# First down group on the up-projection's banks, the sums' matmul six ticks further behind, and the mixers' decay tables behind further projection units

## The chip, the cores and the metric

One Trainium2 chip, one of its eight cores. The metric is the device time of one launch, in microseconds: the median of the runs of one kernel. One more execution was recorded by the profiler; all rows below come from it.

## The reference, cut to what matters

1024 frames of width 1024, with 16 meta tokens in front, go through two layers. The first layer's mixer is a gated DeltaNet ("GDN"), the second's an mLSTM; behind each mixer stands a feed-forward net ("FFN") with a causal convolution over three frames. Everything is float32.

```python
for i in range(DEPTH):                       # DEPTH = 2
    a_in = rms_norm(hs, norm_w[i, 0])
    mix = gated_deltanet(a_in, ...) if i % 2 == 0 else mlstm(a_in, ...)
    hs = hs + keep * rms_norm(mix, norm_w[i, 1])
    f = conv_ffn(rms_norm(hs, norm_w[i, 2]), ...)
    hs = hs + keep * rms_norm(f, norm_w[i, 3])

def gated_deltanet(h, ...):
    proj = h @ w_in                          # 1024 -> q, k, v, z and the gates
    g = -exp(a_log) * softplus(gates + dt_bias)
    G = cumsum(g)                            # the decay table, chunk by chunk
    decay = exp(G_i - G_j)                   # used by every chunk's products
    ...
    return (rms_norm(o, norm_w) * silu(z)) @ w_out

def mlstm(h, ...):
    proj = h @ w_in
    b = cumsum(log_sigmoid(gates))           # its decay table
    ...
    return (rms_norm(hh, norm_w) * o_gate) @ w_out

def conv_ffn(h, w_up, conv_w, conv_b, w_down):
    u = causal_depthwise_conv(h @ w_up, conv_w) + conv_b   # 1024 -> 2 x 2816, 3 taps
    gate, up = u[..., :2816], u[..., 2816:]
    return (silu(gate) * up) @ w_down                      # 2816 -> 1024
```

## The kernel before

**Tiles.** Features lie on the 128 partitions, frames along the free axis. Mixers work on 3 blocks of 348 columns. The out-projections and the FFN work on two halves t = 0 and 1 of 520 columns, each as two quarters n = 0 and 1 of 260. Every product is computed as three matmuls (lines 255 to 257: high part by high, low part by high, high part by low), and each weight tile is split first into its high part by ACT (L145) and its low part by POOL (L146).

**Layers and names.** Tiles of the GDN's out-projection have `go` in their names, those of the mLSTM's `mo`, those of the FFN's down-projection `f` (`dn_f`, `acc_f`, `so_f`), those of its up-projection `up` and `u`. The input of the mLSTM's projection is `xh_f`, `xl_f`, its projections are `pj_mi`, those of the GDN `pj_gi`.

**PSUM.** Eight banks under four tags, two each: `pj`, `pp`, `px`, `sp`. `next_bank` hands them out in turn: with `conv_banks` set it alternates between `pj` and `sp`, otherwise among `pj`, `pp` and `px`. While the up-projection runs, `conv_banks` is set, because the convolution accumulates its outputs `z` in `pp` and `px`: ACT writes the tap with the bias there (L1325), and VectorE adds the other two taps (L1327). An up-projection's bank is emptied into `u` by ACT (L1297) or, in the later columns j, where seven products are combined, by VectorE (L227).

**The FFN.** `ffn()` runs `up()` for 22 column tiles j; for j below 6 only the half t = 0 is computed at first (the plain form, four banks of 24 matmuls: `up_j_h_n`), later both halves together with seven products for eight. Then come the down groups (t, g): (0,0) contracts two tiles of the hidden features, the others four. A group has 16 outputs `dn_f_t_g_m_n`, each in a bank of its own, which VectorE copies (L484, g = 0) or adds (L486) to `acc_f`.

**Ticks and lags.** Work that follows an out- or down-projection is queued as jobs and emitted by `tick()`: a down bank of four tiles advances it by 2, one of the first group by 1, a plain up bank by 4, a bank of the seven-product form by 2, a unit of the mLSTM's projection by 5. At the end of a half's quarter the jobs are: the mean square of the mix (`fs_of`, `fs_ogo`, its rstd on ACT as Ln, L284, and Exp, L287); eight steps, two ticks apart, that add the residual (L378, L379) and accumulate the squares of the new stream in `ss` (L320 on ACT, L321 on VectorE); `LAG_PRE` ticks later the sums' matmul `fs_go`, `fs_mo` or `fs_f` (L328, two fp32 passes with a matrix of ones), and the factor `r` from it; and `LAG_OPS` = 2 ticks later the loads and splits of the next operands (`f_b` loaded in L1249, scaled in L1252, `b` and `t` cast by ACT in L1258 and completed by VectorE in L1259 and L1263). The up-projection reads `b` and `t`.

**Engines are in order.** What stands behind a waiting instruction on an engine waits too. A list scheduler places the emitted work on each engine; the rows under "The change" are its result.

**Decay tables.** In both mixers a generator `gates` computes the gates on VectorE step by step; its last step makes the running sum on TensorE (`cum_gdn`, `tot_gdn`, `cum_ml`, `tot_ml`, L584 and L588). The GDN takes that step before its first activation burst, the mLSTM before its units i = 2 and 3 of the projection.

Of the kernel before, what the change touches and what calls it, by code (L numbers as in the profile page):

```python
# [41 lines left out]

N_FIRST = 6

LAG_POST, LAG_N, LAG_PAGE, LAG_PRE, LAG_OPS = 6, 16, 2, 4, 2

LAST = ("f1", 1)

# [18 lines left out]
def weave(*parts):  # L67

    live = [[g, max(n, 1), 0] for g, n in parts]
    while live:  # L70
        p = min(live, key=lambda p: (p[2] + 0.5) / p[1])
        try:
            next(p[0])
            p[2] += 1
        except StopIteration:
            live.remove(p)


def run(g):
    for _ in g:  # L80
        pass
# [8 lines left out]
class Trunk:  # L90
# [560 lines left out]
    def gdn(self):  # L651
        a = self.a
        self.o_dram = [self.pd.tile([P, 2, TP], F32, tag=f"o_g_{h}", name=f"o_g_{h}", bufs=1) for h in range(NQK)]
        self.pages_of = {}
        self.blocks = {}
        n_all = NQK * NB
        tiles = lambda h: [h, NQK + h, 2 * NQK + 2 * h, 2 * NQK + 2 * h + 1, 32 + 2 * h, 32 + 2 * h + 1]

        def silu(h, tiles):
            self.burst([y for i in tiles for y in self.pages_of[h, i]], self.last, AF.Silu)  # L660

        def project(n):


            h, part = divmod(n, NB)
            i = (4, 0, 2)[part]
            g = h + (part > 0)
            yield from self.gdn_project(g, tiles(g)[i : i + 2], i)
            silu(g, (i, i + 1))

        def enter(b):
            hs = []
            for m in range(KD):
                h = self.page("C", f"hs_in_{b}_{m}", N_PAGES)
                sl = slice(b * BS, (b + 1) * BS)
                nc.sync.dma_start(h, self.hs[:, m, sl])
                self.put_input(h, m, sl)
                hs.append(h)
            return hs

        nc = self.nc
        t0 = tiles(0)
        weights = lambda t: self.split_weights(a["gdn_w_in"][t], f"gi{t}")
        self.new_input(0, "in")
        self.rt = self.new_factors("in")
        wg = self.split_weights(a["gdn_gate_w"], "gdn_gates", 32)
        hs = [enter(0)]
        ws = [weights(t0[0])]
        self.tables()
        hs.append(enter(1))  # L690
        ws.append(weights(t0[1]))
        hs.append(enter(2))
        rows = []
        for b in range(NB):
            acc = self.squares_now(hs[b], f"in{b}", None)
            self.now.append(lambda acc=acc, b=b: self.norm(acc, f"in{b}", self.r(b)))
            rows.append(self.gate_rows(wg, b, "gdn"))
            if b == NB - 1:
                gates = self.gdn_gates(rows)
                next(gates)  # L700
            for i in range(2):
                run(self.gdn_unit(0, i, t0[i], ws[i], b))
        lb, tb = next(gates)
        silu(0, (0, 1))
        order = t0[2:4] + [t for h in range(NQK) for t in tiles(h)[4:] + (tiles(h + 1)[:4] if h + 1 < NQK else [])]
        self.queue_weights([(a["gdn_w_in"][t], f"gi{t}") for t in order], 1)

        def first():
            yield from self.gdn_project(0, tiles(0)[2:4], 2)
            silu(0, (2, 3))  # L710

        weave((self.gdn_prepare(0, tb, lb), 13), (first(), 6))
        out = self.out_projection(a["gdn_w_out"], NQK, "go", GDN_CORE, GDN_LATE, 1, 2)
        for n in range(n_all):
            parts = [(self.gdn_recur(n, tb), 14)]
            if n + 1 < n_all:
                parts.insert(0, (self.gdn_prepare(n + 1, tb, lb), 27))
            if n:
                parts.append((self.gdn_finish(n - 1), 4))
            parts.append((project(n), 8) if n <= n_all - NB else (islice(out, 28), 28))  # L720
            weave(*parts)
        weave((self.gdn_finish(n_all - 1), 4), (out, 30))
# [341 lines left out]
    def mlstm(self):  # L1064
# [16 lines left out]
        for b in range(1, NB):  # L1081
            rows.append(self.gate_rows(wg, b, "ml"))
            if b == NB - 1:
                gates = self.ml_gates(rows)
                next(gates)
            for i in range(2):
                self.ml_unit(0, i, t0[i], ws[i], b)
                self.tick(5)
        li, tb = next(gates)
        self.queue_weights([(a["ml_w_in"][t], f"mi{t}") for t in t0[2:] + [t for h in range(1, ML_H) for t in tiles(h)]], 1)  # L1090
        for i in (2, 3):
            w = self.next_weights()
            for b in range(1, NB):
                self.ml_unit(0, i, t0[i], w, b)

        def first():
            for i in (4, 5):
                w = self.next_weights()
                for b in range(1, NB):
                    self.ml_unit(0, i, t0[i], w, b)  # L1100
                    yield
            self.burst([y for i in (4, 5) for y in self.pages_of[0, i]], self.last, AF.Sigmoid)
# [244 lines left out]
    def ffn(self, L, order, row, post, pre):  # L1347
        nc = self.nc
        name = f"f{L}"
        self.hidden = self.pd.tile([P, NF, NTOK], F32, tag=f"h_{L}", name=f"h_{L}", bufs=1)  # L1350

        src = lambda k, t: self.hidden[:, k, t * HB : (t + 1) * HB]
        place = lambda n: self.fp_page(n, F32R)
        seq = [(t, g) for t in range(2) for g in range(-(-NF // 4))]
        group, queue = self.second(name, NF, self.a["ffn_w_down"][L], src, place, seq, lambda t, n: self.end(t, n, post, pre, name, t == 1 and pre is not None))
        queue()
        while 0 not in self.xo:
            self.tick(1)
        self.hs, self.rt = self.new_hs, self.new_rt
        self.conv_banks, self.evicted = True, None  # L1360
        for j, halves in order:
            if 1 in halves and 1 not in self.xo:
                while 1 not in self.xo:
                    self.tick(1)
            self.up(L, j, halves)
        self.conv_banks = False
        for t, g in seq:
            run(group(t, g))
            if (t, g) == (1, 1) and pre is not None:
                self.new_input(pre, name)  # L1370
                for part in [z for p in self.xt for z in p]:
                    nc.gpsimd.memset(part[:, NTOK:].bitcast(F32), 0.0)
                for m in range(KD):
                    h = self.raw_input(f"hi_{name}_{m}").rearrange("p n c -> p (n c)")
                    nc.sync.dma_start(h, self.new_hs[:, m, :HB])
                    self.put_input(h, m, slice(0, HB))
        self.hs, self.rt = self.new_hs, self.new_rt
# [169 lines left out]
```

## Time and profile before

| | |
|---|---|
| runs, median (lowest to highest of 3) | 3403.2 us (3397.31 to 3404.38) |
| profiled execution, its own time | 3410.23 us |
| its span, first to last instruction | 3408.4 us |
| mean granted TensorE clock | 0.969 of full speed |
| TensorE busy (matmuls) | 3207.7 us, 94% |
| VectorE busy | 2367.7 us, 69% |
| ScalarE busy | 1604.0 us, 47% |
| GpSimd busy | 1672.7 us, 49% |
| DMA | 297.74 MB, mean 87 GB/s |

Busy time is summed over stages that differ: an engine that is half idle over the span may be full in one stage. The two FFNs lie at about 1362 to 2190 us and 2635 us to the end; the GDN before the first, the mLSTM between them.

### The profile page before, as it was taken

The page shows a single profiled execution, that of the slowest core. Times are in us where ns is not written, and L with a number is a line of the kernel's source. Part 1 is how long each engine was busy: PE and PEld are TensorE (multiplying, and loading weights), DVE is VectorE, ACT ScalarE, POOL GpSimd, SP SyncE. Part 2 cuts the span into 40 slices and gives each one's busy share as a digit, 9 for nine tenths or more (in the row PEclk, how much of TensorE's full clock was granted, in tenths as well). Part 3 has the DMA queues.
Part 4 walks back from the last instruction along what each step waited for, and adds up shares of the span by engine and source line. Part 5 has one row for each costly group of instructions (what it writes and reads, how often), then busy time and mean ns, then how long its engine had stood idle before and what let it go on. Part 6 is the DMA issues. An engine that isn't in the chain of part 4 may idle for free.

```text
span 3408.4 us, 68296 instructions
## 1 busy us (share of the span) xinstructions
PE 3207.7 (94%) x25368; PEld 3118.8 (92%) x25368; DVE 2367.7 (69%) x5143; ACT 1604.0 (47%) x3394; POOL 1672.7 (49%) x1890
## 2 busy tenths in 40 slices
PE   8999999999999999799999999899998799999998
PEld 6889988999889899799999999899998799999998
DVE  7777777777767648977777484634469977777464
ACT  5455545555445434755455243333345755554332
POOL 2433444433434344588766434333343588765453
PEclk9999989999989999899999999999999899999999
DMA  3011101010101336432224454211125433224452
GB/s 119 23 37 34 34 26 34 32 34 28 34 26 34 101 102 194 133 100 93 88 79 135 131 178 133 92 42 57 50 74 186 136 102 96 84 85 130 142 163 88
DMA packets 234510, 297.74 MB, mean 87 GB/s; under 512 B 20684, under 2 KB 167104, under 8 KB 234176
## 3 DMA queue, kind: packets, MB, share of 16 engines
q1 hardware_dynamic: 234176, 293.37, 26.6%
q8 instruction: 200, 3.28, 0.4%
q14 instruction: 134, 1.10, 0.1%
HBM read 240.06 MB, written 53.23 MB: 86 GB/s over the span
## 4 chain that ended last, share of the span: by engine, by line
PE 70%; DVE 15%; issue 3%; ACT 3%; DMA 1%; POOL 1%; SPq 0%; POOLq 0%; DVEq 0%; ACTq 0%
PE up L255 7%; PE up L257 7%; PE up L256 7%; PE dn_f L255 5%; PE dn_f L257 5%; PE dn_f L256 5%; PE pj_gi L257 3%; PE pj_gi L256 3%; PE pj_gi L255 3%; PE pj_mi L255 2%; PE pj_mi L257 2%; PE pj_mi L256 2%; PE dn_go L255 1%; PE pp L994 1%; PE dn_go L256 1%
## 5 line engine op out<-in xcount | busy, mean ns | idle before, releaser
L255 PE MATMUL dn_f<-so_f,wh_f 128*128 128x260 f32 x1344 | 387.7, 289 | 17.5 <-ACT z L1325 5.9
L255 PE MATMUL pj_gi<-xh_in,wh_gi 128*128 128x348 f32 x1152 | 394.3, 342 | 5.7 <-ACT wh_gi L145 3.9
L257 PE MATMUL pj_gi<-xh_in,wl_gi 128*128 128x348 f32 x1152 | 396.5, 344 | 0.5 <-POOL wl_gi L146 0.5
L256 PE MATMUL pj_gi<-xl_in,wh_gi 128*128 128x348 f32 x1152 | 393.7, 342 | 0.0
L257 PE MATMUL dn_f<-so_f,wl_f 128*128 128x260 f32 x1344 | 384.8, 286 | 0.8 <-POOL wl_f L146 0.8
L256 PE MATMUL dn_f<-so_f,wh_f 128*128 128x260 f32 x1344 | 384.5, 286 | 0.0
L146 POOL TENSOR_TENSOR wl_f<-wr_f,wh_f 128x512 fp32r<-128x512 f32 x168 | 226.5, 1367 | 247.6 <-PE dn_f L256 108.8
L146 POOL TENSOR_TENSOR wl_u_s<-wr_u,wh_u_s 128x512 fp32r<-128x512 f32 x176 | 244.3, 1391 | 78.8 <-ACT wh_u_s L145 73.6
L255 PEld LDWEIGHTS dn_f<-so_f,wh_f 128*128 128x128 f32 x1344 | 258.3, 192 | 20.2 <-ACT z L1325 6.3
L486 DVE TENSOR_TENSOR acc_f<-acc_f,dn_f 128x260 f32<-128x260 f32 x320 | 133.0, 421 | 194.6 <-PE dn_f L257 193.7
L1327 DVE SCALAR_TENSOR_TENSOR z<-u,fcw,z 128x260 f32<-128x260 f32 x528 | 244.9, 486 | 29.0 <-POOL u L1318 23.0
L257 PEld LDWEIGHTS dn_f<-so_f,wl_f 128*128 128x128 f32 x1344 | 258.5, 192 | 1.1 <-POOL wl_f L146 1.0
L256 PEld LDWEIGHTS dn_f<-so_f,wh_f 128*128 128x128 f32 x1344 | 258.6, 192 | 0.2
L1325 ACT ACTIVATE z<-u,fcb,fcw 128x260 f32<-128x260 f32 x352 | 191.0, 568 | 115.6 <-DVE u L227 114.8
L255 PEld LDWEIGHTS pj_gi<-xh_in,wh_gi 128*128 128x128 f32 x1152 | 222.2, 193 | 8.0 <-ACT wh_gi L145 4.1
L257 PEld LDWEIGHTS pj_gi<-xh_in,wl_gi 128*128 128x128 f32 x1152 | 222.8, 193 | 2.2 <-POOL wl_gi L146 0.9
L256 PEld LDWEIGHTS pj_gi<-xl_in,wh_gi 128*128 128x128 f32 x1152 | 222.4, 193 | 0.6
L146 POOL TENSOR_TENSOR wl_gi<-wr_gi,wh_gi 128x512 fp32r<-128x512 f32 x96 | 132.5, 1381 | 157.9 <-ACT wh_gi L145 150.9
L742 DVE SCALAR_TENSOR_TENSOR gy<-u_g,c_gdn_conv_w_g,gy 128x348 f32<-128x348 f32 x288 | 187.5, 662 | 7.9 <-ACT gy L740 5.4
L145 ACT CAST wh_f<-wr_f 128x512 fp32r<-128x512 f32 x168 | 102.6, 617 | 186.1 <-PE dn_f L256 142.8
L145 ACT CAST wh_u_s<-wr_u 128x512 fp32r<-128x512 f32 x176 | 106.9, 614 | 164.7 <-PE up L257 83.6
L146 POOL TENSOR_TENSOR wl_u_a<-wr_u,wh_u_a 128x512 fp32r<-128x512 f32 x132 | 170.5, 1296 | 14.2 <-ACT wh_u_a L145 13.6
(501 smaller groups left out, 11683.7 us busy)
## 6 DMA issues: line engine op xcount, KB each, us to landing
wr_u<-in_ffn_w_up_dram SPq DMA_DIRECT2D x224, 256.0 KB, 2.6
wr_f<-in_ffn_w_down_dram SPq DMA_DIRECT2D x176, 256.0 KB, 2.7
wr_gi<-in_gdn_w_in_dram SPq DMA_DIRECT2D x96, 256.0 KB, 2.6
h<-y SPq DMA_DIRECT2D x176, 130.0 KB, 2.3
si_f<-h SPq DMA_DIRECT2D x88, 260.0 KB, 3.3
wr_go<-in_gdn_w_out_dram SPq DMA_DIRECT2D x64, 256.0 KB, 2.8
wr_mi<-in_ml_w_in_dram SPq DMA_DIRECT2D x44, 256.0 KB, 2.5
o_g<-gy SPq DMA_DIRECT2D x48, 174.0 KB, 1.8
```

The source lines that it names most:

```text
L145: nc.scalar.copy(hi, part(raw))
L146: nc.gpsimd.tensor_tensor(lo, part(raw), hi.bitcast(F32), ALU.subtract)
L255: nc.tensor.matmul(out, w[0], x[0], start=start, stop=False)
L256: nc.tensor.matmul(out, w[0], x[1], start=False, stop=False)
L257: nc.tensor.matmul(out, w[1], x[0], start=False, stop=stop)
L486: self.evicted = nc.vector.tensor_tensor(acc[m][n], acc[m][n], ps, ALU.add)
L742: ins = nc.vector.scalar_tensor_tensor(y, u[:, j : j + BS], taps[:, j : j + 1], y, ALU.mult, ALU.add)
L994: nc.tensor.matmul(pp[:, c * ne : (c + 1) * ne], ah[:, c, :], ev(X)[:, c], start=True, stop=True)
L1325: nc.scalar.activation(z, p[:, 2 : 2 + QB], AF.Identity, scale=taps[:, 2:3], bias=self.fcb[:, tt : tt + 1])
L1327: nc.vector.scalar_tensor_tensor(z if i or not h else y[h], p[:, i : i + QB], taps[:, i : i + 1], z, ALU.mult, ALU.add)
```

## The change

It has four edits. `LAG_PRE` goes from 4 to 10 ticks. The GDN takes its last gates step after two steps of the weave's projection generator, which then enters the weave with weight 4 and not 6. The mLSTM takes it between units i = 2 and i = 3 and not before both. And `conv_banks` stays set through the first down group, so that (0,0) uses the banks of `pj` and `sp`.

```diff
-LAG_POST, LAG_N, LAG_PAGE, LAG_PRE, LAG_OPS = 6, 16, 2, 4, 2
+LAG_POST, LAG_N, LAG_PAGE, LAG_PRE, LAG_OPS = 6, 16, 2, 10, 2
@@ gdn
-        lb, tb = next(gates)
         silu(0, (0, 1))
 ...
-        weave((self.gdn_prepare(0, tb, lb), 13), (first(), 6))
+        begun = first()
+        for _ in range(2):
+            next(begun)
+        lb, tb = next(gates)
+        weave((self.gdn_prepare(0, tb, lb), 13), (begun, 4))
@@ mLSTM
-        li, tb = next(gates)
         self.queue_weights([(a["ml_w_in"][t], f"mi{t}") for t in t0[2:] + [t for h in range(1, ML_H) for t in tiles(h)]], 1)
         for i in (2, 3):
             w = self.next_weights()
             for b in range(1, NB):
                 self.ml_unit(0, i, t0[i], w, b)
+            if i == 2:
+                li, tb = next(gates)
@@ ffn
-        self.conv_banks = False
         for t, g in seq:
             run(group(t, g))
+            self.conv_banks = False
```

On TensorE, the first down group of the first FFN: the first matmul of each of the first seven outputs (each has six; the names are `dn_f_t_g_m_n`, with a buffer number behind). Before:

```order
L257 MATMUL up_21_1_6_25814<-b_go_1_19287,wl_u_0_21_a_25477 128x260
L255 MATMUL dn_f_0_0_1_0_25935<-so_f_0_0_25888,wh_f_0_0_0_0_25570 128x260
...
L255 MATMUL dn_f_0_0_2_1_25972<-so_f_0_0_25888,wh_f_0_0_1_0_25576 128x260
...
L255 MATMUL dn_f_0_0_4_0_25997<-so_f_0_0_25888,wh_f_0_0_2_0_25582 128x260
...
L255 MATMUL dn_f_0_0_0_0_25919<-so_f_0_0_25888,wh_f_0_0_0_0_25570 128x260
...
L255 MATMUL dn_f_0_0_0_1_25927<-so_f_0_0_25888,wh_f_0_0_0_0_25570 128x260
...
L255 MATMUL dn_f_0_0_1_1_25943<-so_f_0_0_25888,wh_f_0_0_0_0_25570 128x260
```

With the change:

```order
L257 MATMUL up_21_1_6_25814<-b_go_1_19399,wl_u_0_21_a_25477 128x260
L255 MATMUL dn_f_0_0_0_0_25919<-so_f_0_0_25888,wh_f_0_0_0_0_25570 128x260
...
L255 MATMUL dn_f_0_0_0_1_25927<-so_f_0_0_25888,wh_f_0_0_0_0_25570 128x260
...
L255 MATMUL dn_f_0_0_1_0_25935<-so_f_0_0_25888,wh_f_0_0_0_0_25570 128x260
...
L255 MATMUL dn_f_0_0_1_1_25943<-so_f_0_0_25888,wh_f_0_0_0_0_25570 128x260
...
L255 MATMUL dn_f_0_0_2_0_25964<-so_f_0_0_25888,wh_f_0_0_1_0_25576 128x260
...
L255 MATMUL dn_f_0_0_2_1_25972<-so_f_0_0_25888,wh_f_0_0_1_0_25576 128x260
```

The outputs now stand in their own order. On VectorE, before, ten of the last column's L1327 rows stand ahead of the first copy L484 of this group; with the change the first copy stands ahead of 13 of them, and copies and L1327 rows alternate.

On ACT, the first FFN's columns 1 and 2 (`u_2` are copies out of the up-projection's banks, `r_go` the factor of the quarters of t = 1, `b_go` the first casts of the next operands). Before:

```order
L1329 ACTIVATE y_1_0_0_1_19044<-z_1_0_0_1_19045 128x260
L1297 COPY u_2_0_0_0_19083<-up_2_0_0_19087 128x260
L1297 COPY u_2_0_0_1_19085<-up_2_0_1_19124 128x260
L1297 COPY u_2_0_1_0_19084<-up_2_1_0_19156 128x260
L1297 COPY u_2_0_1_1_19086<-up_2_1_1_19186 128x260
L145 CAST wh_u_0_4_0_19067<-wr_u_0_4_0_19059 128x512
L284 ACT_TABLE_LOAD
L284 ACTIVATE r_go<-fs_go_19182,cvals 128x260
L1258 CAST b_go_0_19228<-f_b_go_0_19224 128x520
L287 ACT_TABLE_LOAD
L287 ACTIVATE r_go<-r_go 128x260
L1325 ACTIVATE z_2_0_0_0_19296<-u_2_0_0_0_19083,fcb_17464,fcw_17463 128x260
```

With the change:

```order
L1333 ACTIVATE y_1_0_0_1_19040<-z_1_0_0_1_19041 128x260
L1301 COPY u_2_0_0_0_19079<-up_2_0_0_19083 128x260
L1301 COPY u_2_0_0_1_19081<-up_2_0_1_19124 128x260
L145 CAST wh_u_0_4_0_19063<-wr_u_0_4_0_19055 128x512
L1301 COPY u_2_0_1_0_19080<-up_2_1_0_19156 128x260
L1301 COPY u_2_0_1_1_19082<-up_2_1_1_19182 128x260
L287 ACT_TABLE_LOAD
L287 ACTIVATE r_go<-r_go 128x260
L1329 ACTIVATE z_2_0_0_0_19210<-u_2_0_0_0_19079,fcb_17464,fcw_17463 128x260
...
L284 ACT_TABLE_LOAD
L284 ACTIVATE r_go<-fs_go_19294,cvals 128x260
```

The Exp (L287) that follows the copies of `u_2` is now that of the first quarter; before, it and its table load stood ahead of column 1's `z` rows. The second quarter's Ln comes after column 2's `z` rows, and the first `b_go` cast moves behind three of the copies of `u_3`. Over the whole kernel ACT has two rows more, one table load in each FFN.

On TensorE, the mLSTM's table (`mg_f` are the gates that VectorE makes). Before:

```order
L256 MATMUL pj_mi_1_30069<-xl_f_2_28167,wh_mi_0_30049 128x348
L257 MATMUL pj_mi_1_30069<-xh_f_2_28166,wl_mi_0_30050 128x348
L584 MATMUL cum_ml<-mg_f,c_tri_m 116x36
L588 MATMUL tot_ml<-mg_f,ones_f_69 128x36
L255 MATMUL pj_mi_1_30069<-xh_f_3_28168,wh_mi_0_30049 128x348
```

With the change:

```order
L256 MATMUL pj_mi_2_30080<-xl_f_7_28177,wh_mi_1_30037 128x348
L257 MATMUL pj_mi_2_30080<-xh_f_7_28176,wl_mi_1_30038 128x348
L584 MATMUL cum_ml<-mg_f,c_tri_m 116x36
L588 MATMUL tot_ml<-mg_f,ones_f_69 128x36
L255 MATMUL pj_mi_1_30135<-xh_f_0_28162,wh_mi_0_30045 128x348
```

The two rows now stand 39 matmuls later, behind unit i = 2. `cum_gdn` moves by two matmuls only. The sums' matmul moves, counted in matmuls of the projection: `fs_go` and `fs_mo` of t = 0 by 36 each, of t = 1 by one and a half up banks; `fs_f` in the group (1,1) by 21 for n = 0 and 28 for n = 1; at the start of the mLSTM by 24 for n = 0 and not at all for n = 1, whose jobs are emitted at the end of that stage in any case. On the DMA queue of SyncE the loads `f_b_go_1` (L1249) of t = 0 move behind two more weight loads `wr_u`.

## Rows read from the trace of the kernel before

**Rows 1.** The page: busy time by engine; the chain that ended last, by engine.
```profile
PE 3207.7 (94%) x25368; PEld 3118.8 (92%) x25368; DVE 2367.7 (69%) x5143; ACT 1604.0 (47%) x3394; POOL 1672.7 (49%) x1890
PE 70%; DVE 15%; issue 3%; ACT 3%; DMA 1%; POOL 1%; SPq 0%; POOLq 0%; DVEq 0%; ACTq 0%
```

**Rows 2.** What TensorE waited for, over the span: instruction, what released it, us in total, how often, the longest.
```profile
PE fs_f L328 <- DVE ss_f L321: 13.9, 4, 4.2
PE up L255 <- ACT u L1297: 12.9, 4, 3.9
PE dn_f L255 <- ACT z L1325: 5.9, 2, 3.0
PE fs_go L328 <- DVE ss_go L321: 5.9, 2, 4.4
PE fs_mo L328 <- DVE ss_mo L321: 5.7, 2, 4.1
```

**Rows 3.** Timeline of TensorE through the first down group of the first FFN: start, duration, instruction, in brackets the idle time before it and what ended it. The last row is the first matmul of the next group, (0,1).
```profile
1845.40 0.28 PE L256 MATMUL up<-b_go,wh_u_a 128*128 128x260 f32 x1
1845.52 0.28 PE L257 MATMUL up<-b_go,wl_u_a 128*128 128x260 f32 x1
1846.99 0.36 PE L255 MATMUL dn_f<-so_f,wh_f 128*128 128x260 f32 x1 [1.19 <-ACT so_f L451]
...
1850.93 0.56 PE L255 MATMUL dn_f<-so_f,wh_f 128*128 128x260 f32 x1 [2.97 <-ACT z L1325]
1851.28 0.42 PE L256 MATMUL dn_f<-so_f,wh_f 128*128 128x260 f32 x1
1851.49 0.42 PE L257 MATMUL dn_f<-so_f,wl_f 128*128 128x260 f32 x1
...
1855.50 0.58 PE L255 MATMUL dn_f<-so_f,wh_f 128*128 128x260 f32 x1 [1.63 <-ACT y L1329]
...
1866.89 0.29 PE L255 MATMUL dn_f<-so_f,wh_f 128*128 128x260 f32 x1
```

**Rows 4.** Timeline of VectorE in the same stretch, then the stretch as a window (length, busy time of PE, PEld, DVE, ACT, POOL, granted clock, DMA share, GB/s).
```profile
1846.42 0.42 DVE L227 TENSOR_TENSOR u<-up,u_u 128x260 f32<-128x260 f32 x1
1848.81 0.42 DVE L227 TENSOR_TENSOR u<-up,m_u 128x260 f32<-128x260 f32 x1
1850.36 0.42 DVE L227 TENSOR_TENSOR u<-up,m_u 128x260 f32<-128x260 f32 x1
1851.04 1.67 DVE L1327 SCALAR_TENSOR_TENSOR z<-u,fcw,z 128x260 f32<-128x260 f32 x4
1861.37 1.14 DVE L484 COPY acc_f<-dn_f 128x260 f32<-128x260 f32 x3 [0.17 <-PE dn_f L257]
1845.00:1868.00 23.00, 17.21 (x113) 16.55 (x112) 18.43 (x40) 11.13 (x23) 12.52 (x30) 0.78 0.46 149
```

**Rows 5.** Timeline of TensorE at the sums `fs_f`: two in the group (1,1), two at the start of the mLSTM.
```profile
2007.72 1.23 PE L328 MATMUL fs_f<-ss_f,ones_f 128*128 128x260 f32 x2 [3.99 <-DVE ss_f L321]
2024.00 1.23 PE L328 MATMUL fs_f<-ss_f,ones_f 128*128 128x260 f32 x2 [2.26 <-DVE ss_f L321]
2152.53 0.70 PE L328 MATMUL fs_f<-ss_f,ones_f 128*128 128x260 f32 x2 [4.19 <-DVE ss_f L321]
2169.67 0.71 PE L328 MATMUL fs_f<-ss_f,ones_f 128*128 128x260 f32 x2 [3.50 <-DVE ss_f L321]
```

**Rows 6.** The GDN's out-projection and the start of the first up-projection: TensorE's waits, and the stretch as a window (columns as in rows 4).
```profile
1326.54 1.23 PE L328 MATMUL fs_go<-ss_go,ones_f 128*128 128x260 f32 x2 [4.44 <-DVE ss_go L321]
1342.24 0.71 PE L328 MATMUL fs_go<-ss_go,ones_f 128*128 128x260 f32 x2 [1.45 <-DVE ss_go L321]
1375.03 0.80 PE L255 MATMUL up<-b_go,wh_u 128*128 128x260 f32 x2 [6.80 <-ACT b_go L1258]
1312.00:1396.00 84.00, 64.52 (x480) 62.52 (x478) 81.28 (x156) 41.58 (x93) 34.98 (x26) 0.88 0.42 133
```

**Rows 7.** The first FFN's columns 2 to 4: TensorE's waits, and ACT's first table load and Ln behind the copies `u_2`.
```profile
1417.16 0.71 PE L328 MATMUL fs_go<-ss_go,ones_f 128*128 128x260 f32 x2 [2.38 <-ACT u L1297]
1433.14 0.49 PE L255 MATMUL up<-b_go,wh_u 128*128 128x260 f32 x1 [3.75 <-ACT u L1297]
1448.85 0.39 PE L255 MATMUL up<-b_go,wh_u 128*128 128x260 f32 x1 [2.42 <-ACT u L1297]
1418.48 1.28 ACT L284 ACT_TABLE_LOAD   x1
1419.77 0.48 ACT L284 ACTIVATE r_go<-fs_go,cvals 128x260 f32<-128x260 f32 x1
```

**Rows 8.** Timeline of TensorE at the mLSTM's table (the last two projection matmuls ahead of it, the table, two rows behind it that stand nine matmuls apart), and at the GDN's.
```profile
2189.21 0.32 PE L256 MATMUL pj_mi<-xl_f,wh_mi 128*128 128x348 f32 x1
2189.37 0.32 PE L257 MATMUL pj_mi<-xh_f,wl_mi 128*128 128x348 f32 x1
2192.80 0.39 PE L584 MATMUL cum_ml<-mg_f,c_tri_m 116*116 116x36 f32 x2 [3.12 <-DVE mg_f L1044]
...
2194.72 0.49 PE L257 MATMUL pj_mi<-xh_f,wl_mi 128*128 128x348 f32 x1
...
2197.33 0.49 PE L257 MATMUL pj_mi<-xh_f,wl_mi 128*128 128x348 f32 x1
...
80.96 0.50 PE L584 MATMUL cum_gdn<-gd_g,c_tri_g 116*116 116x144 f32 x2 [3.04 <-DVE gd_g L647]
```

## The prediction, made before the changed kernel ran

> **What bounds the kernel now.** I read the page's busy times and its chain first. TensorE is busy for 3207.7 of 3408.4 us, and the chain that ended last lies on it for 70% and on VectorE for 15% [rows 1]. So matmul time that nobody removes is the bulk, and this change removes none: it can only win from the 200 us in which TensorE stands. The waits of TensorE [rows 2] say who ends that idle time. The largest entry that the change touches are the sums' matmuls `fs_*`, which wait for VectorE's running sum: 13.9 us in four waits for `f`, 5.9 and 5.7 in two each for `go` and `mo`. Then come the up-projection behind ACT's copies `u` (12.9), the first down group behind `z` (5.9), and the two decay tables (3.1 and 3.0, [rows 8]). Then I read the timeline at each of these places, since a wait costs more than its idle time: behind one the matmuls stand 0.22 us apart (1851.28 to 1851.49, [rows 3]) where they otherwise stand 0.12 apart (1845.40 to 1845.52, [rows 3]). That is TensorE at 1.2 GHz instead of 2.4; the stretch of the first down group was granted 0.78 of full speed [rows 4].
>
> **First down group (both FFNs).** From the last up matmul to the next group's first it takes 1866.89 - 1845.52 = 21.4 us [rows 3]. 97 steps of 0.12 are 11.6, so 9.8 us are lost per FFN: 5.8 in three idle waits (1.19, 2.97, 1.63) and the rest at half clock. The cause of two of the waits is that the group's banks `pp` and `px` still hold the last column's `z`. With the change the outputs go to `pj` and `sp`, which VectorE's combines (L227) free at 1846.84, 1849.23 and 1850.78 (start plus duration, [rows 4]); the first output I let follow the last up matmul. So the first four can start at about 1845.6, 1846.9, 1849.3 and 1850.9, and behind 1850.8 VectorE has 16 copies at 0.38 (1.14 for three) and 13 L1327 rows at 0.42 (1.67 for four, [rows 4]), in alternation: 6.1 + 5.5 = 11.6 us, to 1862.4. TensorE's six matmuls per output take 0.72, less than the 0.80 that VectorE takes, so VectorE sets the end: 1866.9 - 1862.4 = 4.5 us gained per FFN, 9 in all. Bounds: if TensorE stays at 1.2 GHz through the other twelve outputs they need 12 x 6 x 0.22 = 15.8 from 1850.9, and 0.2 us is left; if VectorE's tail of z rows falls behind the group, TensorE's own 8.6 us make it 7.3. What loses its cover is the last column's convolution, ACT's `y` and POOL's products: its hidden tile is read only by the last down group.
>
> **Sums in the out-projections (t = 0).** `fs_go` waits 4.44 and 1.45 us [rows 6], `fs_mo` 5.7 in two [rows 2]; 36 matmuls of 0.12 are 4.3 us of cover, so the idle time before them goes. But VectorE is busy for 81.3 of the 84.0 us in this stretch [rows 6], and the up-projection at its end waits 6.80 us for `b_go`, which is the same VectorE chain. TensorE arrives earlier and waits there. At most VectorE's 2.7 idle us can come back; I take 1 per layer, 2 in all. The other end: if the later sum delays the operands in full, +4.3 per layer.
>
> **Sums in group (1,1).** `fs_f` waits 3.99 and 2.26 us [rows 5]. The second sum is complete when VectorE says so, at 2024.0; what the change gives is that 28 matmuls now stand ahead of it instead of behind: 28 x 0.12 = 3.4 us. Bounds: 0 (TensorE waits for evictions in those outputs, since VectorE is what it waited for) and the two waits, 6.2.
>
> **Sums at the mLSTM's start.** The waits are 4.19 and 3.50 us [rows 5]. Only the first sum moves. The time won is lost again at the second, whose place and VectorE chain are the same. I take 0, between +3.8 (24 matmuls at 0.16 of delay for the operands) and -4.2.
>
> **Decay tables.** `cum_ml` waits 3.12 us for VectorE's gates [rows 8], and then ten matmuls run at 0.29 apart (2194.72 to 2197.33) where they were 0.16 apart ahead of it (2189.21 to 2189.37): 1.3 us more. The 39 matmuls now ahead of it cover 6.2 us against the 3.4 from 2189.37 to 2192.80, so the whole 4.4 goes. Bounds: 3.1 (the idle time alone) and 4.4. What reads the table first stands behind still more projection, so its lateness is hidden; if that cover were gone it would cost the 6.2 of the move. `cum_gdn` moves by two matmuls: 0.3 of its 3.04 us [rows 8], with 0 and 3.0 as bounds; the shuffled rows of the GDN's first blocks are counted at nothing because no stage there gains or loses work.
>
> **Up-projection, columns 1 to 5 (t = 1's sums and operands).** TensorE waits here 2.38, 3.75 and 2.42 us behind ACT's copies `u` [rows 7]. ACT's queue is what moves. Ahead of the copies `u_2` there is one table load and one Exp less (1.28 + 0.42), and the casts of the operands stand among the copies of `u_3` and ahead of later ones, where they wait for VectorE. Each FFN gets one table load more. I expect the first two waits to shrink by some 1.7 each and the later ones to grow by about as much as one load: -2 per FFN, -4 in all. Bounds: -8.5 per FFN (all three waits gone) and +4.3 (1.5 up banks, 36 matmuls of 0.12, passed through to the operands).
>
> The Trainium skill ("ScalarE: Activation LUTs", section "What ACT_TABLE_LOAD costs") puts a switch of tables at 1.28 us for the load and 1.38 for a drain. The trace agrees with the load, 1.28 us, but the Ln behind it starts 1.29 us after the load's start [rows 7], so no drain shows here. By the page the extra load of each FFN would cost 2.66 and not 1.28, and the sum would be 2.8 us worse.
>
> **Sum.** -9 - 2 - 3.4 + 0 - 4.4 - 0.3 - 4 = -23.1 us. Against the profiled execution's 3410.23 that is 3387.1. That execution lies 7.0 us above the median, so against 3403.2 it is 3380.
>
> **Rivals.** *TensorE cold in the first down group.* The short outputs wait a little for every bank, and the clock stays at 1.2 GHz. For it: the stretch was granted 0.78 [rows 4], and 1.19 + 2.97 + 1.63 us of waits were enough. Against: the later outputs would follow each other. Then the group gives 0.4 instead of 9: -14.5, 3389. The Trainium skill ("TensorE: Matmul & The Clock Gate", section "A second HAM failure mode: psum-queue depth-cycling") states this very thing: groups of matmuls that cycle through banks with small idle times make the clock swing, although no idle time is long.
>
> *The stalls only move.* VectorE and ACT are the ones waited for, and neither gets less work (ACT gets two loads more). Then only the table (4.4) and part of the group (1,1) remain: about -6, 3397, inside the 6.8 us (0.2%) that a measurement here tells from no change. For it: VectorE's 81.3 of 84 us [rows 6]. Against: in the first down group it is banks, not work, that are short.
>
> *Slower: the later sums reach the operands.* Five chains of operands hang on the moved sums: two halves in two FFNs and the mLSTM's input. If t = 0's are late by 36 matmuls at half clock (7.8 us), t = 1's by 36 at full clock (4.3) and the mLSTM's by 24 (3.8), that is +28.0 against -17.1 from the down groups, (1,1) and the tables: +10.9, 3414. It decides from 3.4 us of lateness per chain; a measurable loss needs (17.1 + 6.8)/5 = 4.8. Against it: `fs` comes later in the order, not in time, wherever TensorE stood at it.
>
> *All of it vanishes.* If copies and sums are all covered, the table's 4.4 and 0.3 are joined by 14.6 in the down groups, 5.4 at the out-projections, 6.2 in (1,1) and 17.0 behind the copies: -48, 3355.
>
> **Chances and range.** The forecast (-16 to -31): 0.50. Cold clock, with other partial gains (-7 to -16): 0.22. Only moved (within 6.8 either way): 0.13. Slower: 0.07. Well beyond the forecast (below -31): 0.08. So faster 0.80, same 0.13, slower 0.07. The range reaches from 3364, half way to the case in which all vanishes, to 3398, which takes in the cold clock and the near end of the case in which stalls move; about 2 in 10 lie outside. For the forecast alone it is 3372 to 3387.
>
> **What would show it.** Right: the group (0,0) ends about 17 us after the last up matmul, with no `z` among TensorE's releasers; `cum_ml` without a wait; one wait less than before at `fs_f` of (1,1), with the second near 2 us or gone; `fs_go` and `fs_mo` of t = 0 without a wait, but `up` behind `b_go` longer, 9 to 12 us. Wrong: that last wait unchanged or gone (then the out-projections gave more), or new waits at columns 4 and 5 of the up-projection of over 4 us each, or `up` behind `t_go` at column 6, which now waits for nothing.

## The result, and the profile after

The changed kernel takes 3376.47 us (median of 5 runs, 3375.09 to 3388.12), against 3397.92 us of the kernel before in the same series: the ratio is 0.9944, with a 95% interval of 0.9927 to 0.9961, or 13 to 25 us faster. The forecast was 3380, 23 us faster. In a second series the same kernel took 3384.13 us (8 runs, 3376.36 to 3392.45) beside 3396.63, ratio 0.9955 (0.9935 to 0.9975). The profiled execution took 3388.12 us, and its span is 3386.3.

The page's busy times of the changed kernel, which answer to [rows 1]:

```profile
PE 3189.9 (94%) x25368; PEld 3101.5 (92%) x25368; DVE 2353.6 (70%) x5143; ACT 1605.1 (47%) x3396; POOL 1662.1 (49%) x1890
```

TensorE's matmuls are the same 25368, yet its busy time is 17.8 us less: fewer of them run at 1.2 GHz (the mean granted clock is 0.974 of full speed and was 0.969). That is why the waits alone mislead. Here are TensorE's waits after the change, which answer to [rows 2]: instruction, releaser, us in total, times, longest.

```profile
PE up L255 <- ACT u L1301: 21.8, 2, 11.0
PE fs_f L328 <- DVE ss_f L321: 12.7, 4, 8.2
PE up L255 <- ACT b_go L1262: 6.8, 1, 6.8
PE dn_f L255 <- DVE u L227: 4.9, 6, 1.4
PE fs_go L328 <- DVE ss_go L321: 3.9, 2, 3.3
PE cum_gdn L584 <- DVE gd_g L647: 3.8, 1, 3.8
PE fs_mo L328 <- DVE ss_mo L321: 3.3, 1, 3.3
```

`cum_ml` and the waits of `dn_f` for `z` are gone. The waits behind the copies `u` went from 12.9 us in four to 21.8 us in two of 11 each.

Since both kernels issue the same matmuls, the times at which the same matmul starts can be subtracted. I took the starts of the first matmul of a stage from each trace, so this table is worked out from the traces (us; the last three columns are explained below):

| stage, between matmul starts | before | after | banks alone | lag alone | lag 7 for t = 1 |
|---|---|---|---|---|---|
| GDN, to the first of its out-projection | 1121.0 | 1116.8 | 1111.7 | 1111.7 | 1104.5 |
| its out-projection | 239.2 | 239.3 | 242.3 | 237.8 | 238.4 |
| first up-projection, through column 6 | 121.8 | 124.9 | 120.7 | 125.1 | 123.4 |
| the rest of it | 363.5 | 363.5 | 363.5 | 363.5 | 363.5 |
| last up matmul to the group (0,1) | 21.4 | 14.8 | 14.4 | 19.5 | 14.4 |
| down groups through the first sum of (1,1) | 147.9 | 142.7 | 146.8 | 142.8 | 142.7 |
| mLSTM, its first 300 projection matmuls | 75.9 | 70.4 | 74.4 | 76.3 | 70.2 |
| second up-projection, through column 6 | 122.6 | 126.1 | 121.1 | 125.7 | 123.6 |
| last up matmul to the group (0,1) | 21.4 | 16.4 | 16.6 | 21.9 | 14.2 |

In this pair of traces the gain comes from four rows: 6.6 and 5.0 us in the first down groups, 5.2 in the down groups through the first sum of (1,1) (4.7 when the second sum is behind TensorE too), 5.5 at the mLSTM's start. It pays back 3.1 and 3.4 us in the up-projections. The GDN's 4.2 us cannot be put down to an edit: kernels with the same order of rows there differ by more (the last section).

The first down group of the first FFN on TensorE, which answers to [rows 3]; its last row is the first matmul of the next group:

```profile
1844.56 0.28 PE L257 MATMUL up<-b_go,wl_u_a 128*128 128x260 f32 x1
1844.67 0.28 PE L255 MATMUL dn_f<-so_f,wh_f 128*128 128x260 f32 x1
...
1846.01 0.39 PE L255 MATMUL dn_f<-so_f,wh_f 128*128 128x260 f32 x1 [0.45 <-DVE u L227]
...
1848.39 0.39 PE L255 MATMUL dn_f<-so_f,wh_f 128*128 128x260 f32 x1 [1.41 <-DVE u L227]
...
1849.95 0.39 PE L255 MATMUL dn_f<-so_f,wh_f 128*128 128x260 f32 x1 [0.56 <-DVE u L227]
...
1859.38 0.28 PE L255 MATMUL dn_f<-so_f,wh_f 128*128 128x260 f32 x1
```

The first output follows the last up matmul, the next three wait for the combines L227 that free `pj` and `sp`, and from 1849.95 nothing waits any more.

The sums `fs_f`, which answer to [rows 5], and the two tables, which answer to [rows 8]:

```profile
2000.22 0.71 PE L328 MATMUL fs_f<-ss_f,ones_f 128*128 128x260 f32 x2 [1.54 <-DVE ss_f L321]
2015.09 0.70 PE L328 MATMUL fs_f<-ss_f,ones_f 128*128 128x260 f32 x2 [2.63 <-DVE ss_f L321]
2140.40 0.71 PE L328 MATMUL fs_f<-ss_f,ones_f 128*128 128x260 f32 x2 [0.35 <-DVE ss_f L321]
2156.52 1.24 PE L328 MATMUL fs_f<-ss_f,ones_f 128*128 128x260 f32 x2 [8.15 <-DVE ss_f L321]
2182.96 0.30 PE L584 MATMUL cum_ml<-mg_f,c_tri_m 116*116 116x36 f32 x2
82.90 0.83 PE L584 MATMUL cum_gdn<-gd_g,c_tri_g 116*116 116x144 f32 x2 [3.82 <-DVE gd_g L647]
```

In (1,1) the first wait shrinks and the second grows a little, 4.2 us in all instead of 6.3. At the mLSTM's start 4.19 + 3.50 became 0.35 + 8.15: what the first sum won, the second gave back.

The new wait, on TensorE, and what ACT and VectorE do ahead of it:

```profile
1458.72 0.59 PE L255 MATMUL up<-b_go,wh_u_a 128*128 128x260 f32 x1 [10.98 <-ACT u L1301]
1447.54 0.39 ACT L1333 ACTIVATE y<-z 128x260 f32<-128x260 f32 x1 [4.68 <-DVE z L1331]
1454.88 1.68 ACT L1262 CAST t_go<-f_b_go 128x520 fp32r<-128x520 f32 x3 [4.86 <-DVE f_b_go L1267]
1458.30 1.21 ACT L1301 COPY u<-up 128x260 f32<-128x260 f32 x4
1414.97 0.89 DVE L1256 SCALAR_TENSOR_TENSOR f_b_go<-f_b_go,c_norm_w_g,r_go 128x260 f32<-128x260 f32 x2 [5.20 <-ACT r_go L287]
1423.99 2.73 DVE L1256 SCALAR_TENSOR_TENSOR f_b_go<-f_b_go,c_norm_w_g,r_go 128x260 f32<-128x260 f32 x4 [4.17 <-ACT r_go L287]
1454.16 0.69 DVE L1267 TENSOR_TENSOR f_b_go<-f_b_go,f_b_go 128x520 f32<-128x520 f32 x1
```

Column 6's first output needs a bank that only a copy of column 5 frees. All four copies run together at 1458.30, behind three casts that waited 4.86 us for VectorE's differences, behind a `y` that waited 4.68 us for VectorE's `z`. VectorE itself had stood 5.20 and 4.17 us for the two factors `r_go` of t = 1. Then it has no room left; as a window (columns as in [rows 4]):

```profile
1424.00:1458.30 34.30, 23.75 (x199) 23.53 (x197) 34.02 (x52) 20.25 (x43) 18.27 (x21) 0.88 0.29 87
```

It is busy for 34.02 of the 34.30 us up to the copies, with the operands' rows and the convolution's. Why the factors come late stands in ACT's queue. Each is a Ln (L284) and an Exp (L287), and here other rows of ACT stand between the two:

```profile
1408.19 0.48 ACT L284 ACTIVATE r_go<-fs_go,cvals 128x260 f32<-128x260 f32 x1
1408.69 1.28 ACT L1333 ACT_TABLE_LOAD   x1
1414.51 0.42 ACT L287 ACTIVATE r_go<-r_go 128x260 f32<-128x260 f32 x1
```

From Ln to Exp it takes 6.3 us for the first factor and 5.3 for the second (1418.20 to 1423.54); before, it took 4.6 and 2.3 (1407.34 to 1411.97, 1419.77 to 1422.08).

### The profile page after: what moved, and what is told of

It reads as the page before. It is cut to its first block, busy times and chain, and to the rows that moved or that the text cites. A ratio compares the mean times of both kernels' runs of the same rounds, so it can differ in the third digit from the quotient of the medians.

```text
span 3386.3 us, 68285 instructions
## 1 busy us (share of the span) xinstructions
PE 3189.9 (94%) x25368; PEld 3101.5 (92%) x25368; DVE 2353.6 (70%) x5143; ACT 1605.1 (47%) x3396; POOL 1662.1 (49%) x1890
## 5 line engine op out<-in xcount | busy, mean ns | idle before, releaser
L255 PE MATMUL dn_f<-so_f,wh_f 128*128 128x260 f32 x1344 | 385.0, 286 | 10.5 <-DVE acc_f L484 5.1
L1331 DVE SCALAR_TENSOR_TENSOR z<-u,fcw,z 128x260 f32<-128x260 f32 x528 | 244.9, 487 | 28.4 <-POOL u L1322 23.1
```

The costliest lines, as they stand in the source:

```text
L255: nc.tensor.matmul(out, w[0], x[0], start=start, stop=False)
L1331: nc.vector.scalar_tensor_tensor(z if i or not h else y[h], p[:, i : i + QB], taps[:, i : i + 1], z, ALU.mult, ALU.add)
```

## The experiments

**Each edit alone on the kernel before.** First the banks, with `self.conv_banks = False` moved into the loop and nothing else:

```diff
-        self.conv_banks = False
         for t, g in seq:
             run(group(t, g))
+            self.conv_banks = False
```

> Before, with conv_banks kept through the first down group and nothing else. Theory A (each edit acts at its own place and the parts add up): the group from the last up matmul to the next group's first takes about 15 us instead of 21.4 in the first FFN and about 16 in the second, as in the changed kernel, and the time falls by 11 to 12 us (6.5 and 5.3); the rest of the trace keeps its steps. Rival B (the short outputs keep TensorE at 1.2 GHz, and the gain in the changed kernel came because TensorE arrived there with other timing): under 4 us in all, with the matmuls of the group 0.22 apart.

Measured: 3383.84 us beside 3398.63, ratio 0.9954 (0.9941 to 0.9967), 11 to 20 us. The groups take 14.4 and 16.6 us, 7.0 and 4.8 less than before. Theory A holds. Rival B falls as the whole story, but the second group still has 18 steps of 0.22 us from one matmul to the next (more on this clock below).

```diff
-LAG_POST, LAG_N, LAG_PAGE, LAG_PRE, LAG_OPS = 6, 16, 2, 4, 2
+LAG_POST, LAG_N, LAG_PAGE, LAG_PRE, LAG_OPS = 6, 16, 2, 10, 2
```

> Before, with LAG_PRE 10 and nothing else. Theory A: -1.4 at the GDN's out-projection, about -1 at the mLSTM's, -5 in the down group (1,1) of the first FFN, -0.6 at the mLSTM's start, and +3 in the columns 1 to 6 of each up-projection, where one wait of about 11 us behind ACT's copies u of column 5 stands in place of three of 2.4 to 4: -1 to -3 us in all. Rival B (the 11 us wait comes from another edit, or from several together): the three waits shrink and no long one appears, and the whole edit gives 8 to 12 us.

Measured: 3398.30 us, ratio 0.9998 (0.9986 to 1.0010). By the trace (column "lag alone") it gains 5.1 us through the first sum of (1,1), 4.6 with the second, and loses 3.2 and 3.1 in the up-projections. The long wait is there (10.96 and 10.85 us), so it is this edit's own, and rival B falls.

The mLSTM's table alone (`li, tb = next(gates)` behind unit i = 2):

> Before, with the mLSTM's table behind unit i = 2 and nothing else. Theory A: the wait of cum_ml (3.1 us) and the half-clock stretch behind it go, -4.5 to -5 us in that place and nothing anywhere else. Rival B (the wait moves to the table's first reader, or to VectorE's rows behind it): 0 to -2 us.

Measured: 3393.84 us, ratio 0.9985 (0.9974 to 0.9995). The mLSTM's first 300 projection matmuls take 71.0 instead of 75.9 us, 4.9 less. No stage behind the GDN has moved by as much; the GDN, whose rows are the same, is 12.2 us shorter in this trace, more than the edit gives. What follows in the mLSTM, up to its out-projection, takes 299.2 us in both traces, so the wait did not move on to the table's readers: theory A holds for the place, and rival B falls.

The GDN's table alone (two steps of `first()`, then `next(gates)`, weight 4):

> Before, with the GDN's table behind two steps of the projection and nothing else. Theory A: cum_gdn still waits 3 to 4 us, the GDN's first blocks change by under 1 us by the trace, and the time is the same within 3 us. Rival B (the new weave helps the first blocks): -2.5 to -4 us up to the first out-projection, where the changed kernel stood 2.7 us earlier than the kernel before.

Measured: 3399.90 us, ratio 1.0004 (0.9995 to 1.0013). No gain is found in the time. `cum_gdn` waits 3.81 us in this kernel's trace, as theory A had it, and not less than the 3.04 of before. The GDN is 6.0 us shorter in this trace, but in four traces with the old order of rows it is 9.3 to 12.2 us shorter, so this says nothing for rival B.

**The lag of t = 1.** The changed kernel, with another lag in that half alone (4 in the first kernel, 7 in the second):

```diff
-                    self.later(LAG_PRE, factors)
+                    self.later(4 if t == 1 and name[0] != "f" else LAG_PRE, factors)
```

> The changed kernel, with LAG_PRE 4 again for the half t = 1 of the two out-projections alone (10 for their t = 0 and for the down-projection). Theory A (the later sums of t = 1 put the operands' chain so late that one wait of 11 us stands at column 6 in place of the three that went): the three waits of 2.4 to 4 us come back, the one of 11 us goes, and each up-projection is 3 to 3.9 us shorter than in the changed kernel, 6 to 8 us in all, so 27 to 29 us under the kernel before. Rival B (the later sums of t = 0, not those of t = 1, push everything back): the 11 us wait stays or moves, and the time is that of the changed kernel within 2 us.

Measured: 3379.42 us beside 3399.31 before, ratio 0.9940 (0.9925 to 0.9955). That is 20 us, not theory A's 27 to 29, and the changed kernel did not run in this series; the time does not tell the two apart. The trace does: the up-projections through column 6 take 120.3 and 123.4 us instead of 124.9 and 126.1, the 11 us wait is gone, and the three short waits are back:

```profile
1413.70 0.70 PE L328 MATMUL fs_go<-ss_go,ones_f 128*128 128x260 f32 x2 [2.15 <-ACT u L1301]
1429.68 0.39 PE L255 MATMUL up<-b_go,wh_u 128*128 128x260 f32 x1 [3.79 <-ACT u L1301]
1445.37 0.39 PE L255 MATMUL up<-b_go,wh_u 128*128 128x260 f32 x1 [2.38 <-ACT u L1301]
```

So the long wait hangs on the later sums of t = 1 and not on those of t = 0. One thing goes with it: this kernel has 78 table loads on ACT, like the kernel before, and the changed kernel has 80.

> The changed kernel, with LAG_PRE 7 for the half t = 1 of the two out-projections (10 elsewhere). Theory A: the chain is 3 ticks, 18 matmuls or 2.2 us, earlier than in the changed kernel, so the wait at column 6 falls from 11 to 7 to 9 us, and part of the earlier waits come back: within 3 us of the changed kernel. Rival B (the wait at column 6 is all or nothing, set by which copies stand behind which casts on ACT and not by the lateness): the wait stays at 10 to 11 us or vanishes.

Measured: 3377.15 us, ratio 0.9936 (0.9918 to 0.9954). The three waits of the first up-projection, last the one at column 6:

```profile
1400.19 1.16 PE L328 MATMUL fs_go<-ss_go,ones_f 128*128 128x260 f32 x2 [2.14 <-ACT u L1301]
1428.05 0.58 PE L255 MATMUL up<-b_go,wh_u 128*128 128x260 f32 x1 [2.58 <-ACT u L1301]
1444.88 0.58 PE L255 MATMUL up<-b_go,wh_u_a 128*128 128x260 f32 x1 [3.73 <-ACT u L1301]
```

The wait at column 6 is 3.7 us, less than theory A's 7 to 9, so it falls faster than the chain is advanced; but it is not all or nothing, as rival B had it. This kernel has 78 table loads too.

**The casts off ACT.** The changed kernel with t = 1's high parts made by VectorE:

```diff
-                nc.scalar.copy(hi, f[o])
+                (nc.vector.tensor_copy if t else nc.scalar.copy)(hi, f[o])
```

> The changed kernel, with the high parts of the operands of t = 1 (14 casts of 128x520 per FFN) made by VectorE and not by ACT. No copy u can then stand behind a cast on ACT. Theory A (the 11 us have two parts: about 5 because the copies of column 5 stand behind casts that wait for VectorE, and about 6 because the operands themselves are late): the first matmul of column 6 no longer waits, a wait of 4 to 9 us for the operands b or t stands one to three outputs later, and each up-projection is 2 to 6 us shorter. Rival B (the place on ACT's queue explains all of it): no wait over 2 us in columns 5 and 6, and 9 to 11 us per up-projection. Rival C (VectorE is the limit, and 14 casts more on it cost what they free): the wait is as long as before or longer, in another place.

Measured: 3384.70 us, ratio 0.9959 (0.9944 to 0.9974). The wait is nearly as long and stands one column earlier. TensorE's row, then ACT's two rows that end it:

```profile
1446.73 0.58 PE L255 MATMUL up<-b_go,wh_u 128*128 128x260 f32 x1 [10.03 <-ACT u L1301]
1446.02 0.39 ACT L1333 ACTIVATE y<-z 128x260 f32<-128x260 f32 x1 [8.74 <-DVE z L1331]
1446.31 1.21 ACT L1301 COPY u<-up 128x260 f32<-128x260 f32 x4
```

With no cast on ACT the copies stand behind a `y` that waits 8.74 us for `z` on VectorE. That fits rival C: the operands' chain on VectorE is late and dense and holds back the convolution's rows; ACT passes it on, because its copies stand behind whatever waits for VectorE. It does not show it alone, since the 14 casts are themselves more work for VectorE.

The traces say why VectorE is late. Counting waits of over 0.3 us between the start of an up-projection and column 6, it stands 9.2 to 9.4 us for the factors `r` in the three traces with the lag of 10 at t = 1 and the casts on ACT (6.7 and 6.9 in this one, where the wait is also there), 1.2 with a lag of 7, and 0.3 to 0.7 with 4. For the loads `f_b` it stands at most 0.4 with 10, and up to 1.9 with 4 or 7. So it is the factor and not the load. How much of the lost time the longer way from Ln to Exp on ACT takes, with its extra table load, and how much the later sum itself, no run here tells apart.

**A better version, and what carries the gain.** The changed kernel again, the one with lag 7 for t = 1 again, and a kernel with the banks and the mLSTM's table alone, in one series:

> The changed kernel again, beside the next two. Both theories: 3375 to 3383 us, and in the trace the stages behind the GDN as in its first profile to within 2 us each (an up-projection through column 6 of 125 to 126 us, the first down group 15 to 16.5 us).

> The changed kernel with LAG_PRE 7 for t = 1 of the out-projections, once more, beside the changed kernel. Theory A (what the first trace showed, 1.5 to 2.5 us less per up-projection and up to 3 elsewhere, is the kernel's own): 3 to 7 us under the changed kernel's median. Rival B (those were the clock's luck): within 2 us of it.

> Before, with two of the four edits: the first down group's banks and the mLSTM's table. Theory A (these two carry the gain; what LAG_PRE gives in the down group (1,1) it takes back in the up-projections, and the GDN's edit gives nothing): 16 to 21 us under the kernel before, within 3 us of the changed kernel. Rival B (the parts add up as the traces of the single edits say, LAG_PRE being worth 2 and the GDN's table up to 4): 3 to 6 us behind the changed kernel.

Measured, beside 3396.63 us before: the changed kernel 3384.13 us, ratio 0.9955 (0.9935 to 0.9975); with lag 7 for t = 1 3374.88 us, 0.9926 (0.9906 to 0.9947); banks and table alone 3379.59 us, 0.9943 (0.9922 to 0.9963). The changed kernel is outside the 3375 to 3383 that was expected of it, and its first down groups take 16.6 and 16.2 us this time. The second trace of lag 7 has 123.5 and 122.7 us through column 6, against 125.4 and 125.9 of the changed kernel beside it. It is 9.3 us ahead of the changed kernel, where theory A had 3 to 7. Its 12 runs in two series have a median near 3375 us, the changed kernel's 13 runs one near 3383, so it has the lowest median of these kernels, though the intervals of the ratios overlap and banks and table alone are only 4.7 us behind. Not all of its lead is the up-projection: 4.3 us of it in the traces are the first down groups (14.3 and 14.2 us), which have at most four steps of 0.22 us there. Whether the lag brings that about is not shown.

The two edits of the last kernel are worth as much as all four (17.0 us, and 4.5 ahead of the changed kernel, with overlapping intervals); `LAG_PRE` = 10 throughout and the GDN's edit add nothing that was measured.

## Why the prediction was right, point by point

The time lies near the forecast, but in part by luck: 21.5 us in the first series, 12.5 in the second. A pair of traces is uncertain by several us in single stages, because the clock differs from one execution to the next. So this table sets the mean of all traces that lack an edit beside the mean of all that have it, stage by stage (us, worked out from the starts of the same matmuls; in brackets the number of values and their range). The two rows of up-projections leave out the traces with another lag at t = 1 or with the casts on VectorE.

| stage | without | with | gain | forecast |
|---|---|---|---|---|
| a first down group, up to (0,1) | 21.0 (8: 19.5 to 21.9) | 15.6 (16: 14.2 to 17.2) | 5.4 each | 4.5 each |
| GDN's out-projection, up to the first up matmul | 241.0 (5: 239.3 to 242.4) | 238.9 (7: 237.8 to 240.9) | 2.1 | 1 |
| mLSTM's out-projection, up to the first up matmul | 131.6 (5: 131.0 to 132.8) | 130.4 (7: 129.7 to 132.6) | 1.2 | 1 |
| from the first matmul of (0,1) to the last of (1,5) | 254.8 (5: 253.5 to 256.1) | 251.6 (7: 251.4 to 253.0) | 3.2 | 3.4 |
| mLSTM, its first 300 projection matmuls | 75.3 (4: 74.4 to 76.3) | 70.4 (8: 69.5 to 71.2) | 4.8 | 4.4 |
| first up-projection, through column 6 | 121.2 (5: 120.7 to 122.0) | 125.1 (3: 124.9 to 125.4) | -3.9 | 2 |
| second up-projection, through column 6 | 122.6 (5: 121.1 to 124.1) | 125.9 (3: 125.7 to 126.1) | -3.3 | 2 |
| GDN, to its out-projection | 1112.6 (5: 1108.8 to 1121.0) | 1113.7 (7: 1104.5 to 1117.8) | -1.1 | 0.3 |

Without the GDN, whose difference is far inside its range, the gains add up to 15 us. All terms but one came out within 2 us; the up-projections missed by 11.2.

**First down group: right on the banks, wrong on what sets the end, too small.** Forecast 9 us, measured 6.6 + 5.0 in the changed kernel and 7.0 + 4.8 alone. The replay of the banks held to 0.1 us (forecast: first four outputs at 1845.6, 1846.9, 1849.3, 1850.9; measured, with everything 0.96 us earlier: 1844.67, 1846.01, 1848.39, 1849.95). From there TensorE waits for nothing, so TensorE and not VectorE sets the end. The term that was mis-sized is VectorE's pace: I took the grouped rows' 0.38 and 0.42 us, 0.80 per output, but rows start on VectorE before the one ahead ends. Behind a copy the next row starts 0.34 us later, behind a L1331 row 0.39 later, as these rows show, and 0.73 per output is TensorE's own 0.72:

```profile
1849.81 0.41 DVE L484 COPY acc_f<-dn_f 128x260 f32<-128x260 f32 x1
1850.15 0.48 DVE L1331 SCALAR_TENSOR_TENSOR z<-u,fcw,z 128x260 f32<-128x260 f32 x1
1850.54 0.75 DVE L484 COPY acc_f<-dn_f 128x260 f32<-128x260 f32 x2
```

In the traces two rows of the last column's L1327 (L1331 in the changed kernel) stand ahead of the first copy and 14 behind it, in both kernels. The section on the change counts ten ahead of it before; what the edit changes is that the copies no longer stand behind twelve of them in one piece.

**The cold clock in that group** was a rival at 22%. In the changed kernel's windows (columns as in [rows 4]) the first group was granted 1.00 of full speed and the second 0.90, with the same three waits (0.45, 1.41, 0.56 and 0.48, 1.38, 0.57):

```profile
1844.50:1859.50 15.00, 12.58 (x101) 11.95 (x100) 14.75 (x35) 9.49 (x19) 11.00 (x28) 1.00 0.60 195
3103.00:3120.00 17.00, 14.57 (x104) 13.94 (x103) 15.51 (x35) 9.85 (x20) 11.04 (x16) 0.90 0.55 176
```

In the eight traces of kernels with these banks, six of the 16 groups take 14.2 to 14.8 us and have at most four steps of 0.22 us from one matmul to the next; the other ten take 15.6 to 17.2 us and have 11 to 18 such steps. So the rival came about in part, in most of the groups, and costs 1 to 3 us each, not the 8.6 that I gave it in all. The Trainium skill ("TensorE: Matmul & The Clock Gate", section "A second HAM failure mode: psum-queue depth-cycling") says that groups that cycle through banks with small idle times make the clock swing; ten of the groups show a swing and six none. What decides between them stays open.

**Sums in (1,1): right in size, not in the sign that I named.** The lag alone gave 4.6 us in its trace and 3.2 in the mean of the traces, for a forecast of 3.4. I expected one wait less and the second near 2 us; both are there, 1.54 and 2.63. Idle time fell by 2.1 us; the rest is what I had left out of the term, the matmuls at half clock behind the waits. The granted clock around them was 0.80 of full speed before (first window, columns as in [rows 4]) and 0.93 after (second):

```profile
2004.00:2030.00 26.00, 20.02 (x127) 19.42 (x128) 22.27 (x43) 10.55 (x23) 8.73 (x10) 0.80 0.65 209
1997.00:2021.00 24.00, 19.83 (x146) 19.29 (x146) 22.49 (x45) 12.50 (x27) 11.24 (x12) 0.93 0.74 236
```

**Sums at the mLSTM's start: right.** 0.35 and 8.15 us instead of 4.19 and 3.50: won and given back, as forecast.

**The mLSTM's table: right.** 4.4 forecast, 4.9 measured in the kernel that has it alone and 4.8 in the mean.

**The out-projections: right in size, wrong in the signs that I named.** I took 1 us per layer. The GDN's gave nothing in the first pair of traces (239.2 to 239.3 us), 2.1 in the mean; the mLSTM's gave 1.2. But I expected `fs_go` without a wait and `up` behind `b_go` with a longer one, and named that last wait unchanged as a sign of being wrong. It is unchanged, 6.8 us. The step "the idle time before them goes" failed: the first `fs_go` waits 0.66 us instead of 4.44, but the second 3.26 instead of 1.45, since VectorE's running sum ends 3.1 us later, counted from the start of the out-projection.

**The up-projections: wrong.** I forecast 4 us less and the changed kernel lost 6.5. The step that failed is "the later ones to grow by about as much as one load": I counted the table loads that moved on ACT, but not what the copies stand behind, nor that VectorE would stand 9.4 us for the factors and the convolution's rows come late behind it. In place of three waits of 2.4 to 3.8 us there is one of 11. The bound of +4.3 per FFN held (3.1 and 3.4), and the rival "the later sums reach the operands" was this mechanism at one of its places. The extra table load of each FFN is not priced here: it is there in every trace with the long wait (80 loads) and in none with a lag of 4 or 7 at t = 1 (78).

**The GDN's table: right that it gives next to nothing.** The 0.3 us do not show: `cum_gdn` waits 3.8 us instead of 3.04.

The sum hides two misses of opposite sign. From the first matmul of the GDN's out-projection to the kernel's last, the changed kernel is 17.6 us faster by the traces, 5.5 less than the 23.1 of the sum: against the forecast 6.5 + 4 = 10.5 us were lost in the up-projections, and some 5 won in the down groups and at the mLSTM's start. The means of the traces give 15. The runs' 21.5 us in the first series and 12.5 in the second lie around that; the second series falls short of the forecast's own -16 to -31.

## What to carry to other kernels

When a short stage stands still because its buffers are still in use by the stage before, give it the buffers that come free first: that gave 5.4 us per stage in the mean here, with no work removed. A lag that hides a wait delays everything behind it in the same queue of jobs: set it where the wait is (7 for t = 1, 10 elsewhere was the best tried) and look for the next in-order engine whose buffer-freeing rows stand behind the delayed chain. Subtract the starts of the same matmul in the two traces rather than compare tables of waits: idle time and the half clock behind it appear together in that difference. Take several traces of each kernel, since one stage moves by 2 us and more from one execution to the next.

## What the runs showed of the hardware

The 13 runs of the changed kernel spread over 17 us, and most of such a spread can arise in the GDN, which three of the four edits leave as it is. With one and the same order of rows it took 1121.0 us in the kernel before, 1111.7 in two others, 1109.8 in the one with banks and table and 1108.8 in the one with the mLSTM's table alone. The place is seen in a window. First the kernel before, then the one with the mLSTM's table, each with the two waits of TensorE that both have there (`px` for `Z`) and matmuls that follow each other in the stretch behind:

```profile
425.00:465.00 40.00, 36.76 (x246) 34.33 (x244) 26.42 (x63) 15.63 (x36) 13.76 (x18) 0.79 0.07 25
441.55 0.37 PE L968 MATMUL px<-i,Z 116*116 116x116 f16 x3 [1.35 <-DVE Z L965]
443.85 0.55 PE L968 MATMUL px<-i,Z 116*116 116x116 f16 x3 [1.24 <-DVE Z L965]
...
458.73 0.49 PE L256 MATMUL pj_gi<-xl_in,wh_gi 128*128 128x348 f32 x1
459.02 0.49 PE L257 MATMUL pj_gi<-xh_in,wl_gi 128*128 128x348 f32 x1
```

```profile
425.00:465.00 40.00, 36.76 (x313) 34.60 (x312) 31.01 (x76) 18.54 (x46) 13.93 (x19) 0.96 0.08 25
442.13 0.37 PE L968 MATMUL px<-i,Z 116*116 116x116 f16 x3 [1.36 <-DVE Z L965]
444.44 0.37 PE L968 MATMUL px<-i,Z 116*116 116x116 f16 x3 [1.24 <-DVE Z L965]
...
447.50 0.49 PE L255 MATMUL pj_gi<-xh_in,wh_gi 128*128 128x348 f32 x1
447.79 0.49 PE L256 MATMUL pj_gi<-xl_in,wh_gi 128*128 128x348 f32 x1
...
450.12 0.32 PE L255 MATMUL pj_gi<-xh_in,wh_gi 128*128 128x348 f32 x1
450.27 0.32 PE L256 MATMUL pj_gi<-xl_in,wh_gi 128*128 128x348 f32 x1
```

The waits are alike to 0.01 us, but in one execution the clock was granted at 0.79 of full speed and 246 matmuls fit into 40 us, in the other at 0.96 and 313. In both TensorE falls to 1.2 GHz behind the second wait: projection matmuls stand 0.29 us apart. In the first they still do at 459.02, 15 us after that wait; in the other they are back at 0.15 at 450.27, 6 us after it. In the five traces with this order of rows, 40 us around this place were granted 0.79, 1.00, 0.83, 0.96 and 0.83 (before, banks alone, lag alone, table alone, banks and table), and around the next place with the same two waits, some 140 us later, 0.96, 0.79, 1.00, 0.96 and 1.00. So two waits of 1.3 us close together are followed by a long stretch at 1.2 GHz, by a short one or by none, with the same rows. Across this place the starts of the same matmuls shift by up to 7.7 us against the kernel before, as much as any edit here gained in one place. What decides it stays open, and taking those waits away was not tried.
